# A two-layer decoder trunk on one core: turnings' splits ahead of queries' evictions in layer B, both halves of the o split on GpSimd, and a reordered start

## The chip, the core and the metric

The kernel runs on one core of one Trainium2 chip. The metric is the device time of one execution in microseconds; of three runs the median is 1007.33 (1006.78 to 1008.36). Positions in the program are told in microseconds from the start of the span of one profiled execution.

## What is computed

The reference, cut to what matters here (batch 1, 512 tokens, 1024 features, float32; `three` products below replace each float32 product):

```
layer A: h = x @ w_in                       # 384 query, 256 key-value, 64 rotary columns
         c_q, c_kv = rmsnorm of the parts;  q = c_q @ w_uq;  q_r = rope(rotary columns of q)
         latent attention, 8 heads, causal;  y = o @ w_o
shared:  k, v = x @ kv_w_shared             # 4 key heads of 64 columns, once
layer B: q = x @ w_q                        # 16 heads of 64 columns
         s = q k^T / 8 + bias[head], window of 128 keys, blocks of 128 queries x 256 keys
         m = max(s, sink); p = exp(s - m) / (sum + exp(sink - m)); o = p v; y = o @ w_o
each:    x = LN(sqrt(2) x + y);  x = LN(sqrt(2) x + mlp(x)),  mlp = relu(x w_up)^2 w_down, 4096 wide
```

## The kernel before

Float32 operands are written as a high half (rounded to the type that TensorE takes at full rate) and a low half, the remainder. `split` makes both: ScalarE copies the source to the high half (line 77), VectorE, or GpSimd where the caller names it, subtracts (line 80). A product is three matmuls (`three`): high with high, high with low, low with high. All matmuls are issued by `group` (line 104) in the order in which the code is written, since `pe` keeps an instruction in program order on its engine. ScalarE, VectorE and GpSimd have no such order: a scheduler arranges each engine's queue when the program is built, by when it expects operands and by priority (`tc.high_priority()`), and from then on each queue is fixed. Buffers come from pools by tag: six PSUM banks `mm` for products, two PSUM banks `tr` for transposes, four weight pairs `wh`/`wl`, two landing tiles `raw`. A new tile in a full pool waits until the last reader of the tile that it takes the place of is done.

**The start.** TensorE runs `WARM` matmuls on zeros. x, transposed in memory, comes in 8 chunks of 128 features (`xraw`), chunks 0 and 1 one by one and then in pairs (`load_x`), all by SyncE's queue, and the first key-value weights (`w_kv`, 640 columns for two chunks) come in two halves by ScalarE's queue. ScalarE loads its function table before its first activation. The loop over `kp` (pairs of chunks) then goes over the four blocks of 128 tokens `t` and issues six matmuls for each: three for each of the two chunks.

**The queries' latent in layer A.** After the values' products (`values`), TensorE turns the normed latent (`normed_t`, line 917: 4 transposes for one group of 128 features, to `cq[f]`), two groups after the third block of tokens and the last group after the fourth; then come the keys of head 0 (`head_keys(0)`), and the rotary queries: for each block of tokens nine matmuls over the three groups `r`, evicted by `rope` on VectorE (lines 928 to 932) to `qrot`. `head_queries(0)` follows, then `pair_rotary(0)` (line 1051), which turns `qrot` of all four blocks.

**Layer B's attention** goes head by head. `run_steps` writes TensorE's order: for head `u` the scores of head `u + 2` (S: 8 matmuls), a part of the fill (Q: 12 matmuls of 512 columns, half of the product that makes the queries of two heads; in the last units parts of the output projection `proj` instead), the turning of head `u` (T: 7 transposes, `turn`, lines 1325 and 1327), and the mix of head `u - 1` (M: 8 matmuls, `mix`). What the other engines do for them:

- S: VectorE adds the bias and takes the maximum in four instructions (line 1297, named ISA in the order's rows), then `nb`; ScalarE makes four exponentials (line 1305) and `ri`; VectorE `sm` and the reciprocal `ri`; GpSimd multiplies `p` by it (lines 1312, 1314).
- T: a split of the transposes in two pieces: `pth` by ScalarE, `ptl` by VectorE, 512 columns from the first `tr` bank, 384 from the second. A turning needs both banks of the turning before it read out.
- M: ScalarE copies half to `low` (line 1354), VectorE adds to `o` (line 1355). After every second head `o` is split to `oh` (ScalarE) and `ol` (GpSimd): the input of the projection.
- Q: after its second half the queries are evicted by `query_parts`: two copies on ScalarE (line 1267) and two subtractions on VectorE (line 1269) to `q`, under high priority.
- Weights: the next `w_sq` or `w_so` tile is split, `wh` by ScalarE, `wl` by GpSimd, or by VectorE for the output projection's tiles from the fourth on.

Of the kernel before, what the change touches and what calls it, by code (L numbers as in the profile page):

```python
# [8 lines left out]
F32 = mybir.dt.float32  # L9
# [6 lines left out]
P = 128  # L16
D = 1024
S = 512
# [15 lines left out]
POOL_O, POOL_SO = (0, 2), (0, 1, 2)  # L34
WARM = 10

# [12 lines left out]
def build(tc, nc, io, out):  # L49
    with ExitStack() as top:  # L50
# [34 lines left out]
        def pe(ins):  # L85
            tc.keep_in_program_order(ins)
# [37 lines left out]
        def raw_tile():  # L124
            return wp.tile([P, 1024], F32, tag="raw", bufs=2, name=nm("raw"))
# [749 lines left out]
        with tc.tile_pool(name="mla", bufs=1) as mp:  # L875
# [72 lines left out]
            for kp in range(4):  # L948
                wh, wl = weights("w_kv")
                for t in range(NT):  # L950
                    tk = slice(t * P, (t + 1) * P)
                    for kk in range(2):
                        k, c = 2 * kp + kk, slice(kk * 320, (kk + 1) * 320)
                        group(kvb[t], three(x0.h(k, tk), x0.l(k, tk), wh[:, c], wl[:, c]), k == 0, k == 7)

# [115 lines left out]
            for t in range(NT):  # L1071
                tk = slice(t * P, (t + 1) * P)
                b = bank()
                for r in range(3):
                    wh, wl = ws[r // 2]
                    c = slice((r % 2) * 512, (r % 2 + 1) * 512)
                    group(b, three(cq[r][:, 0, tk], cq[r][:, 1, tk], wh[:, c], wl[:, c]), r == 0, r == 2)
                rope(qrot[t // 2][:, t % 2, :], b, t, H, scratch())
            head_queries(0)
# [115 lines left out]
        with tc.tile_pool(name="swa", bufs=1) as mp:  # L1195
# [55 lines left out]
            def queries(m, part):  # L1251
# [65 lines left out]
            def turn(h, _):  # L1317
# [3 lines left out]
                for k2 in range(2):  # L1321
                    pt = tbank().rearrange("p (a b) -> p a b", a=2)
                    for a in range(2):
                        kb = 2 * k2 + a
                        pe(nc.tensor.transpose(pt[:, a, 0:P], p[:, kb, P:256], ident))  # L1325
                        if kb + 1 < NT:
                            pe(nc.tensor.transpose(pt[:, a, P:256], p[:, kb + 1, 0:P], ident))  # L1327
                    if k2 == 0:
                        split(pth[:, 0:2, :], ptl[:, 0:2, :], pt)
                    else:  # L1330
                        flat = lambda z: z.rearrange("p a b -> p (a b)")
                        c = slice(512, 512 + 384)
                        split(flat(pth)[:, c], flat(ptl)[:, c], flat(pt)[:, 0:384])
                pts[h] = pth, ptl
# [3 lines left out]
            def mix(h):  # L1338
# [155 lines left out]
```

## Time and profile before

| what | value |
|---|---|
| median of three runs | 1007.33 us (1006.78 to 1008.36) |
| the profiled execution | 1006.56 us, its span 1004.4 us |
| busy in the span | PE 986.9, weight loads 889.4, VectorE 774.8, ScalarE 555.4, GpSimd 217.1 us |
| granted TensorE clock, mean | 0.997 |
| chain that ended last | TensorE 93%, VectorE 3%, ScalarE, DMA and issue 1% each |

The profiled execution's own time is 2.2 us over its span and 0.8 us under the median. Busy shares are means over stages. Idle time of TensorE is what counts here, and the view of the waits gives it by who ended it.

### The profile page before, as it was taken

The numbers are of one execution on the slowest core, as the hardware profiler recorded it, in microseconds if no ns is written. First come the engines' busy times: TensorE is split into PE (matmuls) and PEld (weight loads), VectorE is DVE, ScalarE is ACT, GpSimd is POOL, SyncE is SP. The second block draws the span as 40 slices with busy tenths as digits, with TensorE's granted clock in tenths as the row PEclk, the third lists the DMA queues.
The fourth block names the chain that finished last, engine by engine and source line by source line (L and its number), as shares of the span: only waits on it lengthen the run. The fifth ranks groups of instructions, "written<-read, shape, count | busy, mean of one in ns | idle before, by whom it ended". The sixth has DMA issues, their size and how long they took to land.

```text
span 1004.4 us, 15823 instructions
## 1 busy us (share of the span) xinstructions
PE 986.9 (98%) x6108; PEld 889.4 (89%) x6108; DVE 774.8 (77%) x1241; ACT 555.4 (55%) x847; POOL 217.1 (22%) x203
## 2 busy tenths in 40 slices
PE   8999999999999999999999998999999999999997
PEld 8888888998999999998898887889998999998986
DVE  6588867989768779786686678698885986898756
ACT  5457644467547537646146787546763754664620
POOL 1231101121212212210003663312122032122001
PEclk9999999999999999999999999999999999999999
DMA  7431137489889878954132212168798798798422
GB/s 247 143 99 43 64 105 226 99 185 221 152 191 233 164 168 229 222 95 147 63 105 95 85 64 74 61 192 192 181 202 186 163 217 175 160 269 147 112 97 84
DMA packets 60390, 149.55 MB, mean 149 GB/s; under 512 B 5227, under 2 KB 10012, under 8 KB 60316
## 3 DMA queue, kind: packets, MB, share of 16 engines
q0 software_dynamic: 24320, 58.73, 32.9%
q1 hardware_dynamic: 35708, 89.49, 26.8%
q8 instruction: 48, 0.79, 0.3%
q10 hardware_dynamic: 288, 0.33, 0.1%
q14 instruction: 26, 0.21, 0.1%
HBM read 146.41 MB, written 4.22 MB: 150 GB/s over the span
## 4 chain that ended last, share of the span: by engine, by line
PE 93%; DVE 3%; ACT 1%; DMA 1%; issue 1%; POOL 0%; DVEq 0%; POOLq 0%; ACTq 0%
PE mm L104 85%; PE tr L104 5%; PE tr L1135 1%; PE tr L656 1%; DVE mm L1297 1%; PE tr L1325 1%; ACT wh L77 0%; PE tr L1327 0%; DVE q L1269 0%; DVE wl L80 0%; DMA xraw<-in_xT 0%; DMA raw<-in_w_qr 0%; PE tr L430 0%; DVE ptl L80 0%; DMA raw<-in_w_h 0%
## 5 line engine op out<-in xcount | busy, mean ns | idle before, releaser
L104 PE MATMUL mm<-wh,fac 128*128 128x512 f32 (+1 forms) x944 | 292.7, 386 | 0.0
L77 ACT ACTIVATE wh<-wq 128x1024 fp32r<-128x1024 f32 x164 | 173.7, 1060 | 184.6 <-PE mm L104 132.5
L80 DVE TENSOR_TENSOR wl<-wq,wh 128x1024 fp32r<-128x1024 f32 x164 | 199.4, 1220 | 68.5 <-ACT wh L77 67.5
L104 PE MATMUL mm<-xth,wh 128*128 128x256 f32 (+1 forms) x928 | 243.5, 290 | 0.9 <-ACT p L1305 0.9
L104 PE MATMUL mm<-xth,wl 128*128 128x256 f32 (+1 forms) x800 | 233.2, 292 | 0.0
L104 PEld LDWEIGHTS mm<-wh,fac 128*128 128x128 f32 x944 | 176.2, 188 | 35.6 <-DVE fac L80 0.6
L104 PE MATMUL mm<-xtl,wh 128*128 128x256 f32 (+1 forms) x672 | 197.1, 293 | 0.0
L104 PE MATMUL mm<-wl,fac 128*128 128x512 f32 (+1 forms) x472 | 182.3, 386 | 0.0
L104 PEld LDWEIGHTS mm<-xth,wh 128*128 128x128 f32 x928 | 168.6, 192 | 4.3 <-ACT p L1305 1.1
L104 PEld LDWEIGHTS mm<-xth,wl 128*128 128x128 f32 x800 | 153.2, 192 | 2.6
L77 ACT ACTIVATE wh<-raw 128x1024 fp32r<-128x1024 f32 (+4 forms) x85 | 84.9, 1000 | 100.8 <-PE mm L104 58.1
L199 POOL DMA_DIRECT2D wq<-in_up x64 | 77.5, 1228 | 257.9 <-DVE wl L80 191.8
L104 PEld LDWEIGHTS mm<-xtl,wh 128*128 128x128 f32 x672 | 128.7, 191 | 3.0
L80 DVE TENSOR_TENSOR wl<-raw,wh 128x1024 fp32r<-128x1024 f32 (+3 forms) x65 | 77.9, 1205 | 35.8 <-ACT wh L77 35.3
L104 PEld LDWEIGHTS mm<-wl,fac 128*128 128x128 f32 x472 | 88.8, 188 | 16.5
L199 POOL DMA_DIRECT2D wq<-in_down x48 | 42.0, 875 | 187.6 <-DVE wl L80 181.7
L80 POOL TENSOR_TENSOR wl<-raw,wh 128x1024 fp32r<-128x1024 f32 (+2 forms) x20 | 41.4, 2078 | 86.4 <-ACT wh L77 79.1
L104 PE MATMUL mm<-wh,oh 128*128 128x512 f32 x128 | 51.0, 399 | 0.0
L104 PE MATMUL mm<-wh,ol 128*128 128x512 f32 x128 | 50.1, 392 | 0.0
L104 PE MATMUL mm<-wl,oh 128*128 128x512 f32 x128 | 49.9, 390 | 0.0
L391 POOL TENSOR_TENSOR rs<-mv,half 128x1 f32<-128x1 f32 x16 | 11.0, 689 | 167.0 <-DVE mv L412 166.9
L556 DVE TENSOR_TENSOR x<-mm,x 128x512 f32<-128x512 f32 (+1 forms) x49 | 32.9, 674 | 15.5 <-PE mm L104 15.4
(216 smaller groups left out, 1831.9 us busy)
## 6 DMA issues: line engine op xcount, KB each, us to landing
wq<-in_up POOLq DMA_DIRECT2D x64, 512.0 KB, 8.4
wq<-in_down POOLq DMA_DIRECT2D x48, 512.0 KB, 6.9
wq<-in_up SPq DMA_DIRECT2D x32, 512.0 KB, 7.9
raw<-in_down SPq DMA_DIRECT2D x28, 512.0 KB, 6.7
wq<-in_down SPq DMA_DIRECT2D x24, 512.0 KB, 6.4
raw<-in_up SPq DMA_DIRECT2D x16, 512.0 KB, 5.2
raw<-in_w_o SPq DMA_DIRECT2D x8, 512.0 KB, 4.6
raw<-in_w_sq SPq DMA_DIRECT2D x8, 512.0 KB, 3.3
```

The costliest lines, as they stand in the source:

```text
L77: high = nc.scalar.activation(dst_h, src, AF.Copy)
L80: low = (engine or nc.vector).tensor_sub(dst_l, src, f32(dst_h))
L104: pe(nc.tensor.matmul(dst, st, mv, start=first and i == 0, stop=last and i == len(pairs) - 1, **kw))
L199: nc.gpsimd.dma_start(half(a, jp), chunk(*more, jp), accum_op=ALU.add)
L391: nc.gpsimd.tensor_tensor(r, v, half, ALU.pow)
L556: nc.vector.tensor_add(xs[t][:, c], b, xs[t][:, c])
L656: pe(nc.tensor.transpose(pt[:, a, :], xs[t][:, k * P : (k + 1) * P], ident))
L1135: pe(nc.tensor.transpose(pt[:, kb * P : (kb + 1) * P], p[:, kb * P : (kb + 1) * P], ident))
L1297: nc.vector.tensor_tensor_reduce(out=b[:, a, lo_c:], in0=b[:, a, lo_c:], in1=bias[h // 2][:, h % 2, lo_c:], op0=ALU.add, op1=ALU.max, scal ...
L1325: pe(nc.tensor.transpose(pt[:, a, 0:P], p[:, kb, P:256], ident))
```

## The change

Five edits.

1. Start: `WARM` is 8. Chunk 0 of x goes by SyncE's queue, followed there by both halves of the first weights; chunk 1 goes by ScalarE's queue, behind a one-column activation on zeros, ahead of which the function table is loaded.
2. The loop over the key-value weights issues, for `kp` below 3 and chunk by chunk, first the high-by-high matmuls of all four blocks of tokens, then low-by-high, then high-by-low; the last `kp` goes block by block as before.
3. The turning of the third latent group stands behind `head_keys(0)`, and the rotary queries of blocks 0 and 1 do groups 0 and 1 first.
4. Layer B: `turn`'s splits have high priority, `query_parts` has none.
5. Layer B: GpSimd makes `oh` too (a copy), and for the last pair of heads ScalarE and VectorE make the split.

```
-WARM = 10
+WARM = 8
...
+        dummy = cp.tile([P, 1], F32, name="dummy")
...
+        def fetch_x(k, n, queue):
+            pe(queue.dma_start(xraw[k // 4][:, k % 4 : k % 4 + n, :], io["xT"][:, k : k + n, :]))
...
-            pe(nc.sync.dma_start(src, io["xT"][:, k : k + n, :]))
+            if k > 1:
+                fetch_x(k, n, nc.sync)
...
-        at_hand[0] = raw_tile()
-        fetched.add(0)
-        for c in (slice(0, 320), slice(320, 640)):
-            pe(nc.scalar.dma_start(at_hand[0][:, c], io["w_kv"][0][:, c]))
+        fetch_x(0, 1, nc.sync)
+        pe(nc.scalar.activation(dummy, f32(zeros[:, 0:1]), AF.Copy))
+        fetch_x(1, 1, nc.scalar)
...
+                if kp < 3:
+                    for kk in range(2):
+                        for i in (0, 2, 1):
+                            for t in range(NT):
+                                group(kvb[t], [terms(t, kk)[i]], kp == kk == i == 0, False)
+                else:
+                    for t in range(NT):
+                        group(kvb[t], terms(t, 0) + terms(t, 1), False, True)
...
-                if t >= 2:
+                if t == 2:
                     with tc.high_priority():
-                        normed_t(qn, range(2) if t == 2 else range(2, 3), gq, cq)
+                        normed_t(qn, range(2), gq, cq)
             head_keys(0)
+            with tc.high_priority():
+                normed_t(qn, range(2, 3), gq, cq)
...
-            for t in range(NT):
+            qb = {}
+            for t, rs in ((0, (0, 1)), (1, (0, 1)), (0, (2,)), (1, (2,)), (2, range(3)), (3, range(3))):
...
-                    with tc.high_priority():
-                        query_parts(m, slice(0, S), b)
+                    query_parts(m, slice(0, S), b)
...
+                    with tc.high_priority():
+                        if k2 == 0:
+                            split(pth[:, 0:2, :], ptl[:, 0:2, :], pt)
...
-                    split(oh[m // 4][:, m % 4, :], ol[m // 4][:, m % 4, :], o, nc.gpsimd)
+                    high, low = oh[m // 4][:, m % 4, :], ol[m // 4][:, m % 4, :]
+                    if m < 7:
+                        nc.gpsimd.tensor_copy(high, o)
+                        nc.gpsimd.tensor_sub(low, o, f32(high))
+                    else:
+                        split(high, low, o)
```

TensorE's order in layer B is the same in both kernels. What moves there is the queues of VectorE, ScalarE and GpSimd. VectorE before, in the steady part of layer B, from the third bias instruction of a head's scores (`mm_1010_6128`) on; `q_999` and `q_1000` are a pair's queries, `ptl_1002` the low half of the turning that stands before these scores on TensorE:

```order
L1297 ISA mm_1010_6128<-mm_1010_6128,bias_966_5936 128x256
L1297 ISA mm_1010_6128 128x1
L1297 ISA mm_1011_6133,mm_1010_6128<-mm_1011_6133,bias_966_5936 128x256
L1297 ISA mm_1010_6128 128x1
L1269 TENSOR_TENSOR q_999_6090<-mm_984_6007,q_999_6090 64x512
L1269 TENSOR_TENSOR q_1000_6091<-mm_984_6007,q_1000_6091 64x512
L1297 ISA mm_1011_6133,mm_1010_6128<-mm_1011_6133,bias_966_5936 128x256
L1297 ISA mm_1010_6128 128x1
L80 TENSOR_TENSOR ptl_1002_6097<-tr_1003_6098,pth_1001_6096 128x512
L80 TENSOR_TENSOR ptl_1002_6097<-tr_1004_6105,pth_1001_6096 128x384
```

VectorE at the same place with the change:

```order
L1314 ISA mm_1011_6133,mm_1010_6128<-mm_1011_6133,bias_966_5936 128x256
L1314 ISA mm_1010_6128 128x1
L1314 ISA mm_1011_6133,mm_1010_6128<-mm_1011_6133,bias_966_5936 128x256
L1314 ISA mm_1010_6128 128x1
L80 TENSOR_TENSOR ptl_1002_6097<-tr_1003_6098,pth_1001_6096 128x512
L1327 TENSOR_TENSOR sm_993_6049<-sm_993_6049,ri_994_6050 128x4
L1318 TENSOR_SCALAR nb_1007_6125<-mm_1010_6128,sink8_155 128x4
L1286 TENSOR_TENSOR q_999_6090<-mm_984_6007,q_999_6090 64x512
L1286 TENSOR_TENSOR q_1000_6091<-mm_984_6007,q_1000_6091 64x512
L80 TENSOR_TENSOR ptl_1002_6097<-tr_1004_6105,pth_1001_6096 128x384
```

The 512 columns of the turning's low half moved ahead of the two query subtractions and behind the fourth bias instruction; the 384 columns stayed behind the query subtractions.

ScalarE before, at the same place, from the copy `low` of a mix on (`p_997` are exponentials, `wh_1014` a weight tile of the output projection):

```order
L1354 ACTIVATE low_991_6045<-mm_990_6036 64x512
L1305 ACTIVATE p_997_6066,sm_993_6049<-mm_995_6051,nb_992_6048 128x128
L1305 ACTIVATE p_997_6066,sm_993_6049<-mm_995_6051,nb_992_6048 128x256
L1305 ACTIVATE p_997_6066,sm_993_6049<-mm_996_6056,nb_992_6048 128x256 x2
L1309 ACTIVATE ri_994_6050<-nb_992_6048,sink_148 128x4
L77 ACTIVATE wh_1014_6154<-raw_1013_6153 128x1024
L1267 ACTIVATE q_999_6090<-mm_984_6007 64x512
L1267 ACTIVATE q_1000_6091<-mm_984_6007 64x512
L77 ACTIVATE pth_1001_6096<-tr_1003_6098 128x512
L77 ACTIVATE pth_1001_6096<-tr_1004_6105 128x384
```

ScalarE with the change:

```order
L1373 ACTIVATE low_991_6045<-mm_990_6036 64x512
L77 ACTIVATE wh_1014_6154<-raw_1013_6153 128x1024
L1284 ACTIVATE q_999_6090<-mm_984_6007 64x512
L1322 ACTIVATE p_997_6066,sm_993_6049<-mm_995_6051,nb_992_6048 128x128
L1322 ACTIVATE p_997_6066,sm_993_6049<-mm_995_6051,nb_992_6048 128x256
L1322 ACTIVATE p_997_6066,sm_993_6049<-mm_996_6056,nb_992_6048 128x256 x2
L77 ACTIVATE pth_1001_6096<-tr_1003_6098 128x512
L1326 ACTIVATE ri_994_6050<-nb_992_6048,sink_148 128x4
L1284 ACTIVATE q_1000_6091<-mm_984_6007 64x512
L77 ACTIVATE pth_1001_6096<-tr_1004_6105 128x384
```

The weight tile's high half and the first query copy moved ahead of the exponentials.

In layer A, around the third latent group (`cq2`), ScalarE before (`wh_114` is the weight tile of head 1, `kk_116` are the keys of head 0):

```order
L919 ACTIVATE cq_23_168<-tr_110_581,gq_144 128x512
L77 ACTIVATE vh_101_539<-mm_111_588 128x512
L919 ACTIVATE cq2_169<-tr_112_597,gq_144 128x512
L77 ACTIVATE wh_114_605<-raw_113_604 128x640
L77 ACTIVATE kk_116_610<-mm_117_611 128x512
```

and with the change:

```order
L923 ACTIVATE cq_23_168<-tr_110_581,gq_144 128x512
L77 ACTIVATE vh_101_539<-mm_111_588 128x512
L77 ACTIVATE kk_115_603<-mm_116_604 128x512
L77 ACTIVATE wh_113_598<-raw_112_597 128x640
L923 ACTIVATE cq2_169<-tr_117_613,gq_144 128x512
```

`cq2` moved behind the keys of head 0 and behind the high half of head 1's weights.

More of the change, by code (lines that the diff above doesn't have):

```diff
@@ L949, in build, with terms @@
                 wh, wl = weights("w_kv")
-                for t in range(NT):
-                    tk = slice(t * P, (t + 1) * P)
+                def terms(t, kk):
+                    k, tk, c = 2 * kp + kk, slice(t * P, (t + 1) * P), slice(kk * 320, (kk + 1) * 320)
+                    return three(x0.h(k, tk), x0.l(k, tk), wh[:, c], wl[:, c])
+                if kp < 3:
                     for kk in range(2):
-                        k, c = 2 * kp + kk, slice(kk * 320, (kk + 1) * 320)
-                        group(kvb[t], three(x0.h(k, tk), x0.l(k, tk), wh[:, c], wl[:, c]), k == 0, k == 7)
+                        for i in (0, 2, 1):
[4 more added lines that the diff above has]
+                        group(kvb[t], terms(t, 0) + terms(t, 1), False, True)
             def bias_bands():
@@ L1327, in turn @@
                             pe(nc.tensor.transpose(pt[:, a, P:256], p[:, kb + 1, 0:P], ident))
[L1328 to L1333, printed above, removed]
+                    with tc.high_priority():
+                        if k2 == 0:
+                            split(pth[:, 0:2, :], ptl[:, 0:2, :], pt)
+                        else:
+                            flat = lambda z: z.rearrange("p a b -> p (a b)")
+                            c = slice(512, 512 + 384)
+                            split(flat(pth)[:, c], flat(ptl)[:, c], flat(pt)[:, 0:384])
                 pts[h] = pth, ptl
```

12 lines of the change are left out of this document (7 added, 5 removed).

## Prediction

> **What bounds the kernel now.** I read the page first, then the waits of TensorE, then stretches, then the timeline of each engine where TensorE waits. The page's first row says that TensorE is the bound:
>
> ```profile
> PE 986.9 (98%) x6108; PEld 889.4 (89%) x6108; DVE 774.8 (77%) x1241; ACT 555.4 (55%) x847; POOL 217.1 (22%) x203
> ```
>
> So only time in which TensorE stands still, or runs at a lower clock, can be won. In the view of the waits, cut to TensorE, one row is longer than all others together (us in total, times, longest):
>
> ```profile
> PE tr L1325 <- DVE ptl L80: 5.4, 5, 3.3
> ```
>
> These are layer B's turnings (T), waiting for the `ptl` of the turning before. The view by stretches says how little lies elsewhere (columns: length, then busy time of PE, PEld, DVE, ACT, POOL with counts, PEclk):
>
> ```profile
> 197.00:500.00 303.00, 303.00 (x1939) 276.70 (x1938) 236.10 (x258) 169.07 (x175) 55.91 (x54) 1.00 0.77 175
> ...
> 555.00:640.00 85.00, 78.67 (x495) 69.32 (x495) 60.97 (x200) 63.94 (x186) 47.40 (x40) 0.98 0.19 65
> ...
> 610.00:620.00 10.00, 6.47 (x44) 5.60 (x43) 7.93 (x18) 6.58 (x17) 3.34 (x4) 0.95 0.17 53
> 620.00:630.00 10.00, 10.00 (x61) 9.14 (x60) 7.10 (x29) 7.43 (x27) 4.77 (x6) 0.88 0.01 2
> ```
>
> The MLP has no gap. Layer B's attention has 6.3 us, and a lower clock at its end: 5% of 10 us and 12% of 10 us, 1.7 us. Both belong to the longest wait, 3.3 us, after which the clock fell.
>
> **How one wait of a turning comes about.** TensorE, VectorE and ScalarE in one head (S scores, Q query product, T turning):
>
> ```profile
> 588.27 0.27 PE L104 MATMUL mm<-skh,q 128*128 128x128 f32 x1
> ...
> 591.78 0.39 PE L104 MATMUL mm<-xth,wl 128*128 128x512 f32 x1
> 592.99 0.30 PE L1325 MATMUL tr<-ident,p 128*128 128x128 f32 x1 [0.82 <-DVE ptl L80]
> ```
> ```profile
> 588.98 0.30 DVE L1297 CUSTOM_DVE_ANT_0 mm<-mm,bias 128x128 f32<-128x128 f32 x1 [0.24 <-PE mm L104]
> ...
> 590.38 1.39 DVE L1269 TENSOR_TENSOR q<-mm,q 64x512 fp32r<-64x512 f32 x2
> 591.80 0.43 DVE L1297 CUSTOM_DVE_ANT_0 mm<-mm,bias 128x256 f32<-128x256 f32 x1
> ...
> 592.15 1.15 DVE L80 TENSOR_TENSOR ptl<-tr,pth 128x512 fp32r<-128x512 f32 x2
> ...
> 594.05 0.22 DVE L1301 TENSOR_SCALAR nb<-mm,sink 128x4 f32<-128x4 f32 x1
> ```
> ```profile
> 563.41 1.06 ACT L77 ACTIVATE wh<-raw 128x1024 fp32r<-128x1024 f32 x1 [1.92 <-PE mm L104]
> ...
> 586.26 0.37 ACT L1305 ACTIVATE p<-mm,nb 128x128 f32<-128x128 f32 x1 [0.33 <-DVE ri L1311]
> ...
> 588.15 1.06 ACT L77 ACTIVATE wh<-raw 128x1024 fp32r<-128x1024 f32 x1
> 589.10 1.20 ACT L1267 ACTIVATE q<-mm 64x512 fp32r<-64x512 f32 x2
> 590.32 0.98 ACT L77 ACTIVATE pth<-tr 128x512 fp32r<-128x512 f32 x2
> ```
>
> S starts at 588.27, its first bias instruction 0.71 later. Three of them take 1.40, the two query subtractions 1.42, the fourth bias instruction 0.35, and T starts 0.84 after `ptl` does (0.60 of work, the rest the release): 4.72 after S. TensorE was ready at 591.78 + 0.23 = 592.01, 3.74 after S. The wait is 0.98, start to start. The same sum, made with the orders of the other turnings, gives 0.4, 1.0 and, behind a weight split, 3.9: together 6.2, which is the 5.4 of the waits' row and some 0.15 each between the modelled end of a matmul and the place where the next would have started.
>
> **The change in layer B.** In the new order VectorE does, after S: four bias instructions (1.75), `ptl`'s 512 columns (0.60), `sm` and `nb` (0.35), the queries (1.42), and only then `ptl`'s 384 columns (0.55). The second half of T needs those: 0.71 + 1.75 + 0.60 + 0.35 + 1.42 + 0.55 + 0.24 = 5.62 after S, and TensorE comes to it 3.74 + four transposes (0.44) = 4.18 after S. The wait is 1.4, not 1.0. It can't be earlier, as the bias instructions wait for S. ScalarE is no help: the weight tile's copy now stands ahead of the exponentials, and its buffer comes free when Q is done, as the row at 563.41 shows (1.92 idle, ended by TensorE). So ScalarE idles some 2.5 us per pair, which eats the 0.6 of `oh` that it lost. The three pair turnings, summed alike from their orders: the first has `sm`, `ri` and the queries ahead of the 384 columns, 5.8 against 4.2: 1.6; the second 1.4; the third has the queries ahead of both pieces, 5.3 against 3.7, and 0.1 more in its second half: 1.6.
>
> The fourth, the long one, on TensorE and, below, on VectorE:
>
> ```profile
> 610.22 0.27 PE L1325 MATMUL tr<-ident,p 128*128 128x128 f32 x1
> ...
> 614.02 0.39 PE L104 MATMUL mm<-wh,ol 128*128 128x512 f32 x1
> 617.75 0.30 PE L1325 MATMUL tr<-ident,p 128*128 128x128 f32 x1 [3.34 <-DVE ptl L80]
> ```
> ```profile
> 612.80 2.31 DVE L80 TENSOR_TENSOR wl<-raw,wh 128x1024 fp32r<-128x1024 f32 x1
> ```
>
> The split `wl` of 2.31 and two query subtractions stood ahead of `ptl`. Now they stand ahead of the scores' bias instructions, so they start earlier. Counted from the end of Q: ScalarE makes `wh` (0.95), the queries (1.20), two exponentials (0.8; four and `ri` take 588.15 - 586.26 = 1.89), `pth` (0.6): 3.55. VectorE in that time does `wl` (1.3 by the 640-column row below), the queries and one bias instruction, until 3.9, then `ptl`: T at 4.7, its second half at 5.7. TensorE is ready at 614.25 - 610.22 = 4.0. Wait 0.7 and 0.6: 1.3 in place of 3.9, so the clock, which stayed at 1.00 through waits of 0.8, keeps it.
>
> GpSimd gains `oh`'s copy. Its rows:
>
> ```profile
> 0.74 0.63 POOL L342 MEMSET zeros<- 128x640 f32 x1 [0.29 <-POOLq L1483]
> ...
> 595.28 1.29 POOL L80 TENSOR_TENSOR ol<-o,oh 128x512 fp32r<-128x512 f32 x1 [2.21 <-ACT oh L77]
> 597.76 0.40 POOL L1312 TENSOR_TENSOR p<-p,ri 128x128 f32<-128x128 f32 x1 [1.18 <-ACT low L1354]
> 598.12 1.47 POOL L1314 TENSOR_TENSOR p<-p,ri 128x768 f32<-128x768 f32 x1
> ```
>
> Its price lies between a fill of that width (0.63 x 512 / 640 = 0.5) and a two-input subtraction (1.29); I take 0.9, in between, as a copy reads one input. The Trainium skill (GPSIMD Engine Reference, 4.1 Engine selection) calls GpSimd about half as fast as VectorE for two inputs and roughly line-rate for one. By that it would be near the 0.5, and the sum 0.4 better; no run here shows this copy yet. One copy matters: it stands ahead of a multiply (1.87) that a turning needs, and waits for an `o` that comes some 2.5 us before that turning: 0.9 + 1.87 + 0.2 - 2.5 = 0.5 lost (0 to 0.9).
>
> Layer B: 6.2 - (1.6 + 1.4 + 1.6 + 1.3) + 1.7 - 0.5 = 1.5 us won.
>
> **The start and layer A.** The first piece of the chain that ended last (start, length), and rows of the first 14 us of the timeline:
>
> ```profile
> 0.75 4.20 DMA xraw<-in_xT
> ```
> ```profile
> 1.67 1.28 ACT L77 ACT_TABLE_LOAD   x1 [1.67 <-PEq L1483]
> 4.96 0.63 ACT L77 ACTIVATE xth<-xraw 128x512 fp32r<-128x512 f32 x1 [2.02 <-DMA xraw<-in_xT]
> ...
> 6.01 0.41 PE L104 MATMUL mm<-wh,xth 128*128 128x320 f32 x1 [0.55 <-ACT wh L77]
> ...
> 7.78 0.41 PE L104 MATMUL mm<-wl,xth 128*128 128x320 f32 x1 [0.30 <-DVE wl L80]
> ...
> 8.36 0.72 ACT L77 ACTIVATE wh<-raw 128x640 fp32r<-128x640 f32 x1
> ...
> 8.62 0.31 PE L104 MATMUL mm<-wh,xth 128*128 128x320 f32 x1
> ...
> 9.63 0.82 DVE L80 TENSOR_TENSOR wl<-raw,wh 128x640 fp32r<-128x640 f32 x1
> ...
> 13.89 0.31 PE L104 MATMUL mm<-wh,xth 128*128 128x320 f32 x1
> ```
>
> Matmuls come every (13.89 - 8.62) / 36 = 0.146. Before, four of the first 24 are done by 7.78, the rest by 10.7, the next 24 by 14.2. In the new loop four matmuls on one split cover the making of the next, and chunk 0 no longer shares the engines with the first weights from the start; I put it 0.5 earlier than the 4.20 above. The first 24 then run without a wait from 5.4 and end at 5.4 + 24 x 0.146 = 8.9. The next 24 meet splits that no edit moves, as chunks 2 and 3 and their weights come behind the same bytes as before, if in another order: `wh` is done at 9.08, `wl` at 10.45. The last 16 of them need that `wl`, so they end at 10.65 + 16 x 0.146 = 13.0 in place of 14.2: 1.2 won, and the 0.5 doesn't enter. The bounds are 0, if chunk 1 lands late, and 1.8, the whole of 10.7 - 8.9, if the splits come earlier too. The two fewer warm matmuls end before data comes and cost nothing. The Trainium skill (DMA: Bandwidth & Descriptors, Issuing engines are not separate DMA queues) says that all queues share the same 16 engines, which speaks against a win from ScalarE's queue as such: by it only the order of the transfers changes. The sum above takes nothing but the order.
>
> The timeline around the rotary queries:
>
> ```profile
> 47.79 0.66 PE L917 MATMUL tr<-ident,p 128*128 128x128 f32 x4 [0.47 <-DVE cq L920]
> ...
> 50.55 0.74 ACT L77 ACTIVATE wh<-raw 128x640 fp32r<-128x640 f32 x1 [1.38 <-DMA raw<-in_w_h]
> ...
> 52.42 0.68 DVE L928 TENSOR_TENSOR qrot<-mm,const 128x512 f32<-128x512 f32 x1
> ...
> 59.76 0.69 DVE L932 TENSOR_TENSOR qrot<-qrot,p 128x512 f32<-128x512 f32 x1
> ```
>
> The late third turning removes a wait of 0.6 here. But its `cq2` on ScalarE now stands behind `wh`, which waits for a DMA: in these times `cq2` is done at 51.8, its low half at 52.5, and only then can the third group of block 0 end (53.0, as TensorE needs 0.23 a matmul). `rope`'s chain on VectorE takes 59.76 + 0.69 - 52.42 = 8.0 and now starts at 53.4, a microsecond later. It ends at 61.5, and `pair_rotary` waits for it; before, it ended at 60.45. So 1.0 is lost (0.6 won, had the DMA landed early, to 1.5 lost). Start and layer A together: 0.2 won.
>
> **Sum.** 1.5 + 0.2 = 1.7 us. From the profiled execution's 1006.56 that gives 1004.9; the median lies 0.77 above that execution, so 1005.6.
>
> **Rivals.** *The turnings' waits go:* the priority does what it says where I see it miss, for instance if ScalarE and VectorE run early enough that the 384 columns don't queue. For it: in 555 to 640 VectorE is busy 61 and ScalarE 64 of 85 us, so there is room. Against: the order. It gives 6.2 + 1.7 + 0.2 = 8.1 less: 999.2. *ScalarE's held weight copy takes the place of the queries:* the exponentials of the head now stand behind `wh`, and all that follows them (`ri`, `sm`, GpSimd's multiply, `pth`, `ptl`) behind those. For it: the row at 563.41, 1.92 us of ScalarE standing still with work behind it; against it: the multiplies stand two units ahead of the turning that reads them. In the fourth turning this queue is longest. If `wl` is blocked again as in the 2.31 and the exponentials come late too, its wait grows from 3.9 to some 5.0 instead of falling to 1.3, and the clock falls as before: layer B then loses 0.6 + 0.4 + 0.6 in the pairs, 1.1 there and 0.5 on GpSimd, 3.2, and with 0.2 from the start the time is 1010.3. It decides from a wait of 3.3 on, where the clock fell. *The start wins nothing,* since chunk 1 lands late behind the table load on ScalarE: 1.2 less won, 1006.8. Against it stands the row of the table load, which ended at 2.95, two microseconds before chunk 0 was there.
>
> **Chances.** The forecast 0.48, turnings freed 0.22, slower rival 0.13, no win at the start 0.17. A measurement of this kernel tells about 0.2%, 2 us, from no change. The forecast's own range is 1003.5 to 1007.5, of which some 0.19 of 0.48 lies over 2 us faster; with the freed turnings faster is 0.41. Slower is 0.15 (0.13, and 0.02 of a start gone wrong), the rest, 0.44, within. The range runs from the freed turnings to the start without a win and a bound of its cost: 998.8 to 1008.2 (0.4 under 999.2, for the copy at its lower bound; 1.4 over 1006.8, for layer A's loss and the multiply's at their upper bounds of 0.5 and 0.4 more, and 0.5 of a turning). It leaves out the slower rival.
>
> **What would show it.** Right: T waits of 1.4 to 1.6 three times with `ptl` of 384 columns behind `q`, one of about 1.3, PEclk 1.00 from 610 to 630; 24 matmuls done by 9 and 48 by 13; `rope`'s chain starting a microsecond after its place. Wrong: T waits under 0.5 (then my order of VectorE isn't what binds), or a clock under 1.00.

## The result, and the profile after

The median of 14 executions is 1006.38 us (1004.33 to 1008.77), that of the kernel before on the same chips 1006.73 (14 executions). The ratio is 0.9995, with an interval of 0.9987 to 1.0004: no change that can be told. The profiled execution took 1005.52 us (1006.56 before), its span 1003.7 (1004.4); it is the fifth fastest of the 14. Two parts won and one lost, as forecast, but none of the three by the forecast amount.

The page's first row, then TensorE's waits of the changed kernel (us in total, times, longest):

```profile
PE 986.4 (98%) x6106; PEld 888.5 (89%) x6106; DVE 775.2 (77%) x1242; ACT 552.5 (55%) x841; POOL 219.3 (22%) x209
```
```profile
PE tr L1342 <- DVE ptl L80: 2.8, 3, 1.3
PE mm L1064 <- DVE qrot L936: 1.6, 1, 1.6
...
PE mm L104 <- ACT p L1322: 1.4, 2, 0.9
PE tr L1342 <- DVE ri L1328: 1.2, 1, 1.2
```

The turnings' waits went from 5.4 to 2.8 + 1.2 (one is listed under `ri`), and the longest of 3.3 is gone. New are 1.6 before the rotary turning (line 1064) and half a microsecond more for a PSUM bank (`ACT p`). The stretches of layer B (length, then busy PE, PEld, DVE, ACT, POOL, PEclk):

```profile
555.00:640.00 85.00, 79.66 (x511) 70.14 (x510) 62.05 (x203) 62.15 (x181) 52.56 (x48) 1.00 0.19 66
610.00:620.00 10.00, 9.25 (x61) 7.83 (x59) 8.67 (x26) 7.27 (x18) 3.06 (x4) 1.00 0.17 62
620.00:630.00 10.00, 10.00 (x69) 9.08 (x69) 7.57 (x32) 6.64 (x25) 6.79 (x9) 1.00 0.01 2
```

PEclk, the share of its full clock that TensorE was granted, is 1.00 where it was 0.95 and 0.88. Where the time went shows best when the start of the same matmul is taken from both timelines:

| matmul | before | after | difference | what the step did |
|---|---|---|---|---|
| 49th product of the start | 14.33 | 13.81 | -0.52 | start |
| first of the rotary queries | 49.67 | 48.36 | -1.31 | third turning moved: 0.8 won |
| last of the rotary turning | 60.51 | 61.59 | +1.08 | products 0.6 longer (half of it waits for `cq`), 1.8 waiting for `qrot` |
| a mix in layer B ahead of the first change there | 576.09 | 577.26 | +1.17 | nothing |
| a mix after the last turning that waited | 638.72 | 637.57 | -1.15 | layer B: 2.3 won |
| first of the second MLP's norm | 662.54 | 661.77 | -0.77 | a wait for the norm: 0.4 lost |

### The profile page after: what moved, and what is told of

The parts are those of the page before. It is cut to its first block, busy times and chain, and to the rows that moved or that the text cites. A ratio compares the mean times of both kernels' runs of the same rounds, so it can differ in the third digit from the quotient of the medians.

```text
span 1003.7 us, 15822 instructions
## 1 busy us (share of the span) xinstructions
PE 986.4 (98%) x6106; PEld 888.5 (89%) x6106; DVE 775.2 (77%) x1242; ACT 552.5 (55%) x841; POOL 219.3 (22%) x209
## 4 chain that ended last, share of the span: by engine, by line
PE 91%; DVE 4%; DMA 2%; ACT 2%; issue 1%; SPq 0%; DVEq 0%; ACTq 0%
PE mm L104 83%; PE tr L104 5%; ACT wh L77 1%; PE tr L660 1%; PE tr L1153 1%; PE tr L1342 1%; DMA raw<-in_w_o 1%; DMA xraw<-in_xT 1%; DMA wq<-in_up 1%; DVE mm L1314 1%; DVE q L1286 1%; DVE wl L80 0%; DVE ptl L80 0%; PE tr L1344 0%; DVE qrot L936 0%
```

## Experiments

Each was timed beside the kernel before on the same chip. That kernel's median was between 1006.66 and 1006.85 beside all runs with an interval, so their medians may also be set against the changed kernel's 1006.38. Two runs are one execution each and have no interval.

**1. The rotary queries' stage as before.**

```
-            head_keys(0)
-            with tc.high_priority():
-                normed_t(qn, range(2, 3), gq, cq)
-            for t, rs in ((0, (0, 1)), (1, (0, 1)), (0, (2,)), (1, (2,)), (2, range(3)), (3, range(3))):
+            for t in range(NT):      # nine matmuls per block; third turning again ahead of head_keys(0)
```

> The changed kernel, with the rotary queries' stage as before: the third latent turning ahead of the keys again, and the token blocks one after the other. In the trace TensorE reached the rotary turning 0.5 us before its old place in the changed kernel and left it 1.1 us behind it, so this stage alone lost 1.6. Theory: the loss is caused there and kept to the end; the span falls from 1003.7 by 1.6 to about 1002.1, and the wait of TensorE for the rotated queries (1.6, one time) is gone. Rival: what the stage loses is taken up by the heads behind it, which wait less when they start later; then the span stays at 1003.2 to 1003.7 although the wait is gone.

Median 1004.82 us, ratio 0.9977 (0.9967 to 0.9986). TensorE left the rotary turning 1.8 us earlier than in the changed kernel, 0.4 of it from the start, whose code is the same. So this edit costs 1.4 by the trace and 1.6 by the medians, and taking it back is what makes the rest of the change measurable. The span of the profiled execution, 1003.4, is in the range that the rival gave, but not for the rival's reason: the heads behind the stage took nothing up (1.8 was still won at 139 us, 1.4 at 638), and 1.1 went only ahead of the second MLP, at a place that the last section shows.

**2. The two low halves held behind the rotary additions.**

```
+            mark = sp.tile([P, 1], F32, tag="mark", bufs=1, name="mark")
+            gate = nc.gpsimd.tensor_copy(mark, qrot[1][:, 1, 0:1])
+            with tc.issue_after(gate.ins):
+                for parts in held:                # low halves of w_h of heads 2 and 3
+                    nc.gpsimd.tensor_sub(*parts)
```

> The changed kernel, with the low halves of two head weights (heads 2 and 3, GpSimd, 640 columns each) queued on GpSimd behind a one-column copy that reads the last rotated query block, so that neither runs while VectorE makes the last two rotary additions. Theory of blocking: these two additions took 2.79 us together where 0.69 each is usual, because GpSimd's subtractions ran at the same time; now they take 1.3 to 1.4 together, the rotary turning ends some 1.4 earlier, span about 1002.3. Rival, the forecast's reason: the chain is late since its start, as the third latent block is late; GpSimd has no part in it, the two additions end at about 61.4 as they did, and the span stays at 1003.7.

The stage in the changed kernel (VectorE's two last rotary additions, GpSimd's two subtractions, TensorE's last rotary turning), and under it with the hold:

```profile
58.74 2.79 DVE L936 TENSOR_TENSOR qrot<-qrot,p 128x512 f32<-128x512 f32 x2
...
57.47 3.52 POOL L80 TENSOR_TENSOR wl<-raw,wh 128x640 fp32r<-128x640 f32 x2 [5.29 <-ACT wh L77]
...
61.59 0.33 PE L1064 MATMUL mm<-ident,qrot 128*128 128x128 f32 x1 [1.61 <-DVE qrot L936]
```
```profile
58.72 1.29 DVE L941 TENSOR_TENSOR qrot<-qrot,p 128x512 f32<-128x512 f32 x2
...
60.08 0.19 POOL L1103 COPY mark<-qrot 128x1 f32<-128x1 f32 x1 [7.92 <-DVE qrot L941]
60.22 3.11 POOL L1106 TENSOR_TENSOR wl<-raw,wh 128x640 fp32r<-128x640 f32 x2
...
60.07 0.33 PE L1069 MATMUL mm<-ident,qrot 128*128 128x128 f32 x1 [0.28 <-DVE qrot L941]
```

The additions take 1.29 instead of 2.79, and TensorE's wait falls from 1.61 to 0.28, though their start (58.72) hasn't moved. The theory of blocking holds; the late start doesn't. The Trainium skill (SBUF — State Buffer, Who interferes with whom) says that a VectorE instruction with two SBUF inputs contends with a GpSimd one that reads SBUF; these rows agree. But the median was 1012.6, ratio 1.0056 (1.0042 to 1.0069): something else cost some 8 us, and it is in the MLPs, where the 512-column products stood 233 ns apart and not 227.7.

**3. The same hold without a new tile** (the copy writes into `dummy`).

> As the run with the two low halves held on GpSimd, but the one-column copy writes into the dummy tile of the start, so no new tile is made and no other tile moves. Theory: the hold itself is good for 1.4 us in layer A, and the 9 us lost in that run came from the places of the tiles that followed the new one (512-column matmuls of the MLP 233 ns apart instead of 227.7). Then these are 227.7 apart again, the two rotary additions take 1.3 together, the span is 1002.0 to 1002.6, the ratio about 0.998. Rival: the hold costs the MLP something through GpSimd or the transfers behind it; then the matmuls stay 233 apart and the span is near 1010.

Median 1004.64, ratio 0.9981 (0.9972 to 0.9991); the products are 227.7 apart again. The span of its profiled execution is 1004.5, as its first 17 products ran at half pace (0.267 us apart and not 0.147; see experiment 9). Counted from the 49th product, that execution won 1.3 up to the rotary turning and lost 0.5 of it again by 78 us. By the medians the hold is worth as much as taking the edit back.

**4 and 5. The tile alone**, behind the weights' splits, and then in front of them; GpSimd fills it once, and nothing reads it.

```
 (4)  mark = sp.tile([P, 1], F32, tag="mark", bufs=1, name="mark")   # small tiles, allocated behind wh and wl
 (5)  mark = cp.tile([P, 1], F32, name="mark")                        # constants, allocated ahead of them
```

> The changed kernel with nothing but the new one-column tile, filled once by GpSimd and not read: every tile allocated behind it lies 32 bytes further on, those in front (the weights' splits) do not. Theory of places: the MLP's 512-column matmuls are 233 ns apart as in the run with the hold, span 1009 to 1011. Rival: the tile is harmless and the hold did it: 227.7 and a span of 1003.7.

> The same unused one-column tile, but allocated ahead of the weights' splits and not behind them: the factors of the MLP lie at the same addresses as in the run with the tile alone (32 bytes past a multiple of 64), the weights' splits now too. Theory of relation: what slows the MLP's 512-column products is that their two operands stand 32 bytes apart modulo 64 (in the kernel before both are at 32, in the changed one both at 0, in the two slow runs one at 0 and one at 32); here they agree again, the products last 386 ns in the profile as in the changed kernel, and the time is 1005 to 1008. Rival: it is the factors' own address; then 392 ns and 1012 to 1015 as with the tile behind.

One execution each: 1014.71 and 1005.56 us. The page's group of the MLP's products, in the changed kernel, with the tile behind and with the tile in front (busy, mean ns of one):

```profile
L104 PE MATMUL mm<-wh,fac 128*128 128x512 f32 (+1 forms) x944 | 292.7, 386 | 0.0
```
```profile
L104 PE MATMUL mm<-wh,fac 128*128 128x512 f32 (+1 forms) x944 | 297.7, 392 | 0.0
```
```profile
L104 PE MATMUL mm<-wh,fac 128*128 128x512 f32 (+1 forms) x944 | 292.7, 386 | 0.0
```

By the addresses in the built programs, the factors (`fac`) lie at the same places in both. What differs is where the weights' splits (`wh`, `wl`) lie beside them. In runs 2 and 4, the slow ones, the splits are at remainder 0 modulo 64 bytes and the factors at 32; in the kernel before and in run 5 both are at 32, in the changed kernel and in run 3 both at 0. So neither address alone decides, and the theory of relation holds for these two operands; splits at 32 with factors at 0 were not tried, and why TensorE minds stays open. The span of run 4, 1012.9, is over the expected range, as there the clock also fell at the rotary turning (last section).

**6. The first transfers as before, with the new order of products.**

```
+        fetch_x(1, 1, nc.sync)
+        for c in (slice(0, 320), slice(320, 640)):
+            pe(nc.scalar.dma_start(at_hand[0][:, c], io["w_kv"][0][:, c]))
         pe(nc.scalar.activation(dummy, f32(zeros[:, 0:1]), AF.Copy))
-        fetch_x(1, 1, nc.scalar)
```

> The changed kernel with the first transfers as before: x's first two chunks on SyncE's queue, the first weights' two pieces on ScalarE's, the dummy activation behind them; the term-by-term order of the first products stays. Theory: it is the place and the mix of the transfers that made x's third and fourth chunk late (its high half began at 8.26 in place of 7.39), and that took two thirds of the win forecast at the start; here it begins at about 7.4 again, 48 products are done by 13.0 to 13.2 and not by 13.8, the span is 0.6 to 0.8 shorter (about 1003.0), although the first product starts at 6.0 and not at 5.0. Rival: the start is bound by the amount of bytes and not by their queues, and the first matmuls' earlier start is what won the 0.5: then 48 are done at 14.0 or later, and the span is 0.3 to 0.5 longer.

ScalarE's split of chunks 2 and 3 and their weights, and the 25th and 49th product, in this run:

```profile
7.09 1.06 ACT L77 ACTIVATE xth<-xraw 128x1024 fp32r<-128x1024 f32 x1 [0.40 <-DMA xraw<-in_xT]
8.06 0.72 ACT L77 ACTIVATE wh<-raw 128x640 fp32r<-128x640 f32 x1
...
9.33 0.75 PE L104 MATMUL mm<-wh,xth 128*128 128x320 f32 x4
...
12.85 0.75 PE L104 MATMUL mm<-wh,xth 128*128 128x320 f32 x4
```

And in the changed kernel:

```profile
8.26 1.06 ACT L77 ACTIVATE xth<-xraw 128x1024 fp32r<-128x1024 f32 x1 [1.23 <-DMA xraw<-in_xT]
9.22 0.72 ACT L77 ACTIVATE wh<-raw 128x640 fp32r<-128x640 f32 x1
...
9.99 0.85 PE L104 MATMUL mm<-wh,xth 128*128 128x320 f32 x4 [0.48 <-ACT wh L77]
...
13.81 0.75 PE L104 MATMUL mm<-wh,xth 128*128 128x320 f32 x4
```

Nothing but the transfers differs, and the 49th product is 0.96 earlier. One execution each would not settle that, as the start varies: in the traces with the change's transfers the 49th came at 13.14 to 13.86, and at 15.04 with half pace. The split of chunks 2 and 3 settles it: it began at 7.59 to 8.30 in the ten traces with the change's transfers, and at 7.09 to 7.39 in the four with the old ones (before, runs 6, 11 and 12). The first theory holds at the place. At the end it holds less: by the third latent group, which waits for a transfer, 0.4 of the 0.96 were given back, and the median is 1006.37, ratio 0.9994 (0.9985 to 1.0003).

**7. The queries' evictions behind the splits of the next turning.**

```
-                    query_parts(m, slice(0, S), b)
+                    (query_parts if m < 2 else lambda *a: late.append(a))(m, slice(0, S), b)
 ...
+                with behind(last):               # at the end of turn(): behind the 384 columns' split,
+                    while late:                  # on ScalarE and on VectorE
+                        query_parts(*late.pop())
```

> The changed kernel, with the evictions of layer B's queries (two copies on ScalarE, two subtractions on VectorE) queued behind both halves of the split of the turning that follows them, on both engines. Theory: what is left of the turnings' waits (1.42, 1.33, 1.38 from one start to the next, and 0.46) is the wait for the 384 columns behind the queries; these waits fall under 0.4 each, layer B is 3 to 4 us shorter, span 1000 to 1001, time ratio about 0.996. Rival: T is held by the scores' bias work and the exponentials, which stay; the waits stay above 0.9 and the span at 1002.5 or more. Second rival: the wait moves, as the query's bank is held longer or the scores wait for the queries; then turnings' waits go, and others of a like size come.

Median 1001.92, ratio 0.9949 (0.9936 to 0.9962). VectorE and TensorE at the first of the turnings that waited, in the changed kernel and under it here:

```profile
581.56 1.39 DVE L1286 TENSOR_TENSOR q<-mm,q 64x512 fp32r<-64x512 f32 x2
...
583.12 0.55 DVE L80 TENSOR_TENSOR ptl<-tr,pth 128x384 fp32r<-128x384 f32 x1
...
582.29 0.27 PE L1344 MATMUL tr<-ident,p 128*128 128x128 f32 x1
583.82 0.30 PE L1342 MATMUL tr<-ident,p 128*128 128x128 f32 x1 [1.26 <-DVE ptl L80]
```
```profile
580.28 0.55 DVE L80 TENSOR_TENSOR ptl<-tr,pth 128x384 fp32r<-128x384 f32 x1
...
581.68 1.41 DVE L1287 TENSOR_TENSOR q<-mm,q 64x512 fp32r<-64x512 f32 x2
...
582.36 0.27 PE L1345 MATMUL tr<-ident,p 128*128 128x128 f32 x1
582.47 0.27 PE L1343 MATMUL tr<-ident,p 128*128 128x128 f32 x1
```

The 384 columns come ahead of the queries, 2.84 us earlier, and TensorE goes from one half of T to the other without a wait. All four turnings' waits are gone, so the queries were what they waited for. The second rival came true at the last pair alone: there the scores waited for the queries (0.9 and 0.3 from start to start). A wait of 1.1 for a PSUM bank ahead of the first pair, which the kernel before had too, went as well.

**8. `oh` back on ScalarE.**

```
-                    if m < 7:
...
-                        nc.gpsimd.tensor_copy(high, o)
-                        nc.gpsimd.tensor_sub(low, o, f32(high))
-                    else:
-                        split(high, low, o)
+                    split(high, low, o, nc.gpsimd)
```

> The changed kernel with the high half of the o split back on ScalarE and only the subtraction on GpSimd, as before; the priorities stay. By the forecast the copy on GpSimd cost 0.5 (a multiply behind it) and took 0.6 off ScalarE that was idle anyway: the span is the same or up to 0.5 shorter, 1003.2 to 1003.7. Rival: ScalarE's queue carries the chain to the turnings (pth behind the exponentials), so 0.6 more in it per pair shows in the turnings' waits: layer B 1 to 2 us longer, span 1004.7 to 1005.7.

Median 1008.75, ratio 1.0015 (1.0004 to 1.0027), 2.4 us over the changed kernel's. The fourth turning, and the stretch after it:

```profile
621.41 0.30 PE L1342 MATMUL tr<-ident,p 128*128 128x128 f32 x1 [1.86 <-DVE ptl L80]
...
620.00:630.00 10.00, 8.59 (x52) 8.14 (x53) 7.59 (x25) 6.98 (x25) 3.27 (x4) 0.83 0.01 2
```

The fourth waits 1.86 in its second half (0.30 in the changed kernel), and the clock falls: from layer B's first mix to its last it takes 83.4, where the kernel before took 83.1 and the changed one 80.8. The rival holds, and was somewhat too low: taking 0.6 us per pair off ScalarE is a necessary part of the change. The profiled execution's span (1007.4) holds another fall of the clock, at the rotary turning.

**9. Ten warm matmuls** (`WARM = 10` in the changed kernel).

> The changed kernel with ten warm matmuls in place of eight, as before. With eight they end at 5.0 us and the first data came at 5.0 to 6.3, and the first products of the traces so far ran at half pace (0.267 us apart in place of 0.147) for 1 to 17 of them: 7 in the changed kernel, 17 where 25 products had started only at 11.5 (the hold in place) and not at 9.5 to 10.0. Theory: the pause between the warm matmuls and the data lets the clock fall back, in some executions for 4 us, and two more warm matmuls close it. Then the first products are 0.147 apart after at most two, the 25th starts at 9.5 to 10.0 and the 49th at 13.3 to 13.8, and the median of the runs falls by 0.3 to 1.0 against the changed kernel's (ratio to before about 0.999). Rival, the forecast's: the two warm matmuls cost and bring nothing; the spread is the transfers' alone and the median stays at 1006.4.

Median 1006.39, ratio 0.9997 (0.9988 to 1.0006): the rival, and the forecast, hold for the time. In the trace no product of the start ran at half pace, where about seven had in the changed kernel, but the 25th started at 9.88, as it waits for the transfer of chunks 2 and 3. This profiled execution showed something else, right behind the wait of 1.61 at the rotary turning (PEclk is the seventh number):

```profile
62.00:64.00 2.00, 2.00 (x6) 1.60 (x7) 0.94 (x2) 1.58 (x3) 0.00 (x0) 0.62 0.68 192
64.00:66.00 2.00, 2.00 (x6) 1.61 (x5) 1.94 (x3) 1.25 (x2) 0.00 (x0) 0.52 0.01 5
```

The clock fell to a half for some 3.4 us, which cost 1.6. The changed kernel's profiled execution has 1.00 there with the same wait. Of its 14 executions, four had a mean clock of 0.996 and took 1007.2 in the mean; the ten with 0.997 to 0.999 took 1006.1. One such fall lowers the mean clock by 0.0017, so the four fit it; where in those executions the clock fell is not on record.

**10. The queries at high priority again.**

```
-                    query_parts(m, slice(0, S), b)
+                    with tc.high_priority():
+                        query_parts(m, slice(0, S), b)
```

> The changed kernel with the queries' evictions at high priority again; the splits' priority and the copy on GpSimd stay. If the splits' priority does the work, layer B is as in the changed kernel (four turnings' waits of 1.4, 1.3, 1.4 and 0.5 and a wait of 0.6 before the fourth, in all 5.2 from start to start, against 6.2 and 1.7 of half clock before). If the lowering of the queries is what shortened the fourth, they stand ahead of the scores' bias work again, the weight split comes behind them and ahead of the turning's split, and the fourth waits 1.5 to 3 with a fall of the clock from 3.3 on: span 1004.7 to 1007.

Median 1011.02, ratio 1.0047 (1.0029 to 1.0065). The fourth turning and the stretch after it:

```profile
622.28 0.35 PE L1343 MATMUL tr<-ident,p 128*128 128x128 f32 x1 [2.13 <-DVE ptl L80]
...
620.00:630.00 10.00, 7.87 (x48) 7.25 (x48) 8.41 (x28) 6.30 (x20) 6.33 (x6) 0.83 0.16 55
```

So without the lowering of the queries layer B is no better than in the kernel before (83.9 us from its first mix to its last, against 83.1); lowering them is, like `oh` on GpSimd, a necessary part. The span (1008.8) is over the range that was expected, as here the clock also fell at the rotary turning (0.65 and 0.50 in the two stretches from 62 to 66).

**11 and 12. All that helped, together:** the transfers of 6, the hold of 3, the queries of 7 for pairs 2 to 6; then the same with ten warm matmuls.

> All that helped, together: the first transfers as before with the new order of products, the two head weights' low halves held behind the rotary additions (no new tile), and the queries' evictions of pairs 2 to 6 behind the splits of the next turning, those of pair 7 as in the changed kernel, since there the scores waited for them (0.9 and 0.3). If the parts add up: 1001.9 less 0.6 at the start, 1.4 in layer A and 1.1 at layer B's end: about 998.8, ratio 0.992. Rival: the stages behind take some of it up, above all the norm ahead of the second MLP, where TensorE waited 0.9 to 1.3 in the two earlier runs that came there sooner: 999.5 to 1000.5.

> All that helped together, with ten warm matmuls in place of eight. With eight, the profiled execution had its first 16 products at half pace, and the 49th started at 14.8 in place of 12.85 with the same transfers. Theory of the pause: it starts at 12.8 to 13.2, the span falls from 999.1 to about 997.3, the median from 1000.5 to 999.0 to 999.8 (only some executions had the pause). Rival: the warm matmuls bring nothing; the median stays at 1000.5.

Medians 1000.53 and 1000.27, ratios 0.9935 (0.9922 to 0.9947) and 0.9934 (0.9921 to 0.9946). Both beat the kernel before and the changed one by 6 us. The parts don't add up fully: 998.8 was expected, and the rival's 999.5 to 1000.5 came. In 11 the start lost 2 us to half pace in the profiled execution (the 49th product at 14.80), in 12 not (13.27), yet the medians differ by 0.3 only, and the 999.0 to 999.8 that the theory of the pause gave did not come. What is left of the waits in 12:

```profile
PE mm L104 <- ACT p L1336: 2.0, 2, 1.0
PE mm L104 <- POOL zeros L347: 1.4, 1, 1.4
PE tr L669 <- DVE x L431: 0.8, 1, 0.8
```

## Why the prediction was right, and where its steps were not

The time is within the range, and the likeliest case, "no change that can be told" (0.44, with faster at 0.41), came. Of the forecast 1.7 us the profiled execution shows 1.04 (1004.9 forecast, 1005.52 measured). The medians show 0.35, too little to be told from nothing; the median is 0.8 over the forecast 1005.6, which had added 0.77 to the profiled time on the word of three executions, where 14 put that difference at 0.17 for the kernel before. That the profiled total came as near as this is in part luck: layer B won 0.8 more than forecast, the start won 0.7 less, layer A lost 0.6 more, and 0.4 went ahead of the second MLP.

**Layer B, turnings: right in mechanism and nearly in size.** The prediction had waits of 1.6, 1.4 and 1.6, because the 384 columns stay behind the queries, and 1.3 at the fourth. From start to start they were 1.42, 1.33 and 1.38, and at the fourth 0.61 for a bank ahead of it and 0.46 in it, 1.07:

```profile
616.40 0.50 PE L104 MATMUL mm<-wh,oh 128*128 128x512 f32 x1 [0.45 <-ACT p L1322]
...
618.87 0.30 PE L1342 MATMUL tr<-ident,p 128*128 128x128 f32 x1 [0.30 <-DVE ptl L80]
```

Run 7 shows the cause: with the queries out of the way these waits are gone. The clock stayed at 1.00, as forecast.

**Layer B, GpSimd and ScalarE: wrong.** The copy, taken at 0.9, took 0.61:

```profile
584.45 0.61 POOL L1379 CAST oh<-o 128x512 fp32r<-128x512 f32 x1 [1.88 <-DVE o L1374]
```

This is nearer to the lower bound of 0.5, with which the Trainium skill's rule went (GPSIMD Engine Reference, 4.1 Engine selection: one input at about line rate). And the 0.5 for a multiply queued behind it wasn't lost: TensorE waited for no multiply. That term and the turnings' 0.7 are 1.2 over the forecast 1.5, of which 0.8 shows in the 2.3 measured: the half clock had cost some 1.5 by the starts of the same matmuls and not 1.7, and 0.2 stays open. The sentence that ScalarE "is no help", since its idle time eats what `oh` frees, failed too: run 8 lost 2.4 by putting `oh` back. The mean idle time of ScalarE said nothing about the fourth turning, where its queue carried the chain.

**Start: right place, over-sized.** Forecast were 24 products by 8.9, 48 by 13.0, 1.2 won; the 25th started at 9.99 and the 49th at 13.81, 0.5 won. The first 24 did run without a wait, from 5.0 on, but about seven of them at half pace, so that they ended at 9.35. The step that failed is "the next 24 meet splits that no edit moves, as chunks 2 and 3 and their weights come behind the same bytes as before". The bytes are the same, but they came more slowly. Stretches of before and, under them, of after (the last number is GB/s):

```profile
5.00:6.00 1.00, 0.45 (x2) 0.03 (x1) 0.37 (x1) 1.00 (x3) 0.00 (x0) 1.00 0.98 392
6.00:7.00 1.00, 0.63 (x2) 0.41 (x3) 1.00 (x3) 0.87 (x2) 0.00 (x0) 1.00 1.06 414
```
```profile
5.00:6.00 1.00, 1.00 (x5) 1.00 (x5) 0.57 (x2) 0.00 (x0) 0.00 (x0) 1.00 0.90 297
6.00:7.00 1.00, 1.00 (x6) 1.00 (x5) 0.30 (x1) 0.96 (x2) 0.00 (x0) 1.00 0.81 292
```

Before, SyncE's queue held x while ScalarE's held the weights' small pieces; now SyncE's holds all but chunk 1. Run 6 put the transfers back and had the 49th product at 12.85, close to the 13.0 of the sum: by that execution the change's own new transfers took two thirds of what the order of products wins. The reason there was not the sum's, though. No product waited for the `wl` that the sum takes as the bound; they ran one behind the other from the first at 5.70. The Trainium skill (DMA: Bandwidth & Descriptors, Issuing engines are not separate DMA queues) says that issuing from several engines saves issuing time alone; here the rate differed too, 292 to 297 GB/s against 392 to 414. Whether that is the number of queues, or the size and order of the pieces in one of them, wasn't tried. That the two fewer warm matmuls cost nothing held in the median (run 9).

**Layer A: right sign, wrong cause.** Forecast was 1.0 lost because `cq2` is late behind the weight copy and `rope`'s chain starts at 53.4, a microsecond behind its place. It started at 52.49, which with the 0.52 won at the start is 0.6 behind its place:

```profile
52.49 0.69 DVE L932 TENSOR_TENSOR qrot<-mm,const 128x512 f32<-128x512 f32 x1 [0.59 <-PE mm L104]
```

The step that failed is that this lateness sets the end of the chain. It costs little: in runs 2 and 3, which hold GpSimd back, the stage lost 0.2 to 0.3 from the 49th product to the last rotary turning. In the changed kernel the chain ended at 61.53 (58.74 + 2.79), since its two last additions, which the new order puts side by side, met GpSimd's subtractions; run 2 shows it. The loss was 1.6. In the kernel before the two met as well, but there GpSimd waited: its two subtractions took 3.67, in place of the 3.11 of run 2, and VectorE's addition at 59.76 its usual 0.69.

```profile
58.22 3.67 POOL L80 TENSOR_TENSOR wl<-raw,wh 128x640 fp32r<-128x640 f32 x2 [5.27 <-ACT wh L77]
```

The forecast also missed what a wait of this length can do to the clock: it had seen the clock stay through 0.8 and fall after 3.3, and behind this wait of 1.6 it fell in four profiled executions (the last section). How much of the 0.86 between the changed kernel's profiled time and its median comes from that is not shown.

**Rivals.** *The turnings' waits go* did not happen, and run 7 shows what it would have been worth: 4.5 us, of which 1.1 is the bank's wait that went with them, and not the 6.4 by which 999.2 lay below the forecast median of 1005.6. *ScalarE's held weight copy takes the place* did not happen: the fourth turning's `wl` took 1.22 and was not blocked. A picture like it, a long fourth wait and a fallen clock, appeared where a part of the change was taken back (runs 8 and 10). *The start wins nothing* was half true, for a reason other than the table load.

## What to carry to other kernels

Where two queues meet at one wait, ask of each instruction ahead of it who needs it and when: the queries' evictions were needed later (but for the last pair's) and stood ahead of a split needed at once, and an explicit order behind that split won 4.5 us on top of the 2.3 that the priorities and the copy had won. Price a moved transfer by what shares its queue, not by its bytes alone. And before a new small tile is blamed or praised for what it does, look at whether it moved other tiles.

## What the runs showed of the hardware

- **Places of operands.** Thirty-two bytes allocated between the weights' splits and the factors made the MLP's 512-column products 392 ns long instead of 386 in the profile, 233 ns apart instead of 227.7, and the kernel 8 us longer (1012.6 in run 2, 1004.64 in run 3); the same bytes in front of both cost nothing (runs 2 to 5).
- **VectorE and GpSimd hold each other up, and either can be the one that waits.** Ahead of the second MLP VectorE starts a 1024-column operation with two SBUF inputs at the moment when GpSimd starts one on a single column. In the changed kernel GpSimd's was done after 0.56 and VectorE's not held up, in run 1 GpSimd waited for VectorE's end:

```profile
659.01 1.31 DVE L419 SCALAR_TENSOR_TENSOR x<-x,mv,gb 128x1024 f32<-128x1024 f32 x1
...
659.06 0.56 POOL L395 TENSOR_TENSOR rs<-mv,half 128x1 f32<-128x1 f32 x1 [0.21 <-DVE mv L416]
```
```profile
658.36 1.28 DVE L419 SCALAR_TENSOR_TENSOR x<-x,mv,gb 128x1024 f32<-128x1024 f32 x1
...
658.42 1.65 POOL L395 TENSOR_TENSOR rs<-mv,half 128x1 f32<-128x1 f32 x1 [0.21 <-DVE mv L416]
```

  By the profile VectorE's starts 0.05 or 0.06 ahead in both, so the starts don't tell which will wait. In run 1 TensorE waited 1.30 behind this place and not 0.25, so that microseconds won ahead of it can be lost in it. GpSimd was held like this in eight of the fourteen profiled executions (runs 1, 2, 4, 5, 7, 8, 9 and 12); in runs 8 and 9 TensorE came late enough not to wait.
- **The clock's memory.** A wait of 1.6 us was followed by 3.4 us at half clock in the profiled executions of runs 4, 8, 9 and 10, and by none in those of the changed kernel and of runs 5, 6 and 7. The Trainium skill (TensorE: Matmul & The Clock Gate, Part 1: The HAM clock gate) tells of a window of about 3.4 us that runs free of the kernel, by which such a difference is a matter of phase; the length agrees, but that idle must last a whole window does not.
